# Output and up projection of a transformer layer in float32: the border between them cut at 128 tokens, the conditioning paced by progress

## The chip, the cores and the metric

The kernel runs on one core of a Trainium2 chip. The metric is device time in microseconds (us) of one execution; the profile's span is the time from the core's first instruction to its last. Five engines work side by side, each in its own program order: TensorE (PE, matrix products), VectorE (DVE), ScalarE (ACT), GpSimd (POOL) and SyncE (SP, which here issues every DMA). They wait for each other through semaphores.

## What is computed

One layer over 256 latent tokens (with 256 context tokens beside them as keys), model width 2048, everything in float32. The part around the change:

```
sh1, sc1, g1, sh2, sc2, g2 = split(silu(c) @ w_ada + b_ada, 6)    # conditioning, 2048 each
merged = g_a * (o_a @ w_br_a) + g_b * (o_b @ w_br_b)              # both attention branches
x = x + g1 * (merged @ w_out)                                     # output projection, 2048 x 2048
z = rms_norm(x, norm2_g) * (1 + sc2) + sh2                        # per token over 2048 columns
u = z @ w_up                                                      # up projection, 2048 x 11264
x = x + g2 * ((silu(conv(u)_a) * conv(u)_b) @ w_down)             # width-3 depthwise conv over tokens
out = rms_norm(x, final_norm_g)
```

The norm between the two projections needs a token's whole row of x, so no product of the up projection can start before all columns of w_out are done for its token.

## The kernel before

Every float32 operand of a large product is split into two parts of the type float32r: `hi`, a rounding cast on ACT, and `lo`, the remainder, a subtraction on DVE (`hi_lo`, `split`). A product is three matrix products, hi with hi, hi with lo and lo with hi (`mm3`). Weights come in DMAs of 1 MB into a ring of four buffers (`raw`), in one fixed order written in the generator `weights()`; `take()` hands out the next split unit and keeps two further units split ahead (`AHEAD`). There are three buffers each for `hi` and `lo`.

The order on PE is the order of the Python code. Small work (norms, softmax, evacuations, conditioning) stands in generators, the lanes of `Pace`, which adds up estimated times while the program is written: after each matmul group `tick` lets a lane take a step when the backlog that it has added up for DVE and ACT is under the lane's limit. The conditioning of sh2, sc2, g1 and g2 is such a lane (`ada_rest`): 64 loads of 1 MB of w_ada, each followed by two DVE instructions of 1024 columns (`acc<-raw,cs,acc`) that add into one row sum `acc`, and per 1024 columns a product with ones that sums over partitions. Fixed limits per stage hold it back, and `hold` stops it after 32 loads (sh2, sc2) until attention is done; g1 then runs while w_out is multiplied, g2 in the up projection.

The output projection (`w_out_group`, two column halves g) holds four PSUM banks: bank b is token tile b // 2 (128 tokens) and column piece b % 2 (512 columns). All four go through the 16 row tiles kt side by side; only the last two row tiles are done bank by bank. Behind the second half stands the border, with DVE and ACT in written order (`manual_schedule`): four times `residual` (times g1, add x, square and sum), `row_scale` (the norm's factor per token, with a power on POOL), `normed`, transposes on PE, and then per row tile `z2`: ACT writes hi, DVE writes `zf` (the same in full float32) and lo. The first 1024 columns of the up projection (`up_first`) form z2 for both token tiles as they go, in products of 256 tokens; all later parts (`up_part`, 512 columns) multiply hi and lo of z2 side by side, 512 columns at a time (`group_W`).

Earlier, at the end of the gate products, `finish(ll)` forces out what is left of the lane that prepares the latents. Its last piece, `prep_kpe`, rotates the shared key on DVE (`kr`, `kt`) and PE transposes the result before the next projection starts.

Of the kernel before, what the change touches and what calls it, by code (L numbers as in the profile page):

```python
# [32 lines left out]


# [4 lines left out]
REST_CI, REST_AFTER, REST_DMA = 1, 6.0, 6.0  # L39
GAPS = (0.0, 4.0, 10.0, 14.0, 14.0)  # L40
# [10 lines left out]
class Pace:  # L51
# [26 lines left out]
    def tick(self):  # L78
# [4 lines left out]
        while moved:  # L83
            moved = False
            for lane in list(self.lanes):
                gen, ready, limit, dma, _ = lane
                if self.pe < ready or self.left["dve"] > limit or self.left["act"] > limit or self.left["dma"] > dma:
# [63 lines left out]
def _build(tc, nc, es, a):  # L151
# [289 lines left out]
    def ada_rest():  # L441
        for vname, v, gslot in (("sh2", 3, None), ("sc2", 4, None), ("g1", 2, "K1"), ("g2", 5, "Y0")):
            for sec in range(2):
                c0 = v * D + sec * 1024
                while taken_raws[0] >= hold[0]:
                    yield 1.0
# [30 lines left out]
                else:  # L477
                    if sec == 0:
                        gb[vname] = slot(gslot, [P, D])
# [10 lines left out]
                if sec == 1:  # L490
                    ada_done.add(vname)
                yield 0.0


    hold, taken_raws = [32], [0]
    rest = ada_rest()


# [138 lines left out]

    def rows4(w, nk, c0):
# [6 lines left out]
    def weights():  # L645
# [28 lines left out]
        for g in range(2):  # L674
            yield from rows2(a["w_out"][0], KT, g * 1024, 1024)
        yield from rows2(a["w_up"][0], KT, 0, 1024)
        for c0 in up_cols[1:]:
# [8 lines left out]
    up_parts = [(0, 0, None)]  # L686
    for g in range(6):
        for half in range(2):
            for sub in range(min(8, FT - 8 * g) // 4):
                if g + half > 0:  # L690
                    up_parts.append((g, half, sub))
    up_cols = [0] + [half * FF + g * 1024 + sub * 512 for g, half, sub in up_parts[1:]]
# [29 lines left out]
    for ci in range(nch - 1):  # L722
# [4 lines left out]
        if ci == REST_CI:  # L727
            pace.add(rest, after=REST_AFTER, limit=REST_LIM, dma=REST_DMA, prio=9)
# [263 lines left out]
    pace.limit(rest, REST_LIM_B)  # L992
# [62 lines left out]
    pace.limit(rest, REST_LIM_Q)  # L1055
# [109 lines left out]
    pace.limit(rest, REST_LIM_A)  # L1165
# [3 lines left out]
    hold[0] = 48  # L1169
    pace.limit(rest, REST_LIM_W)  # L1170
# [27 lines left out]
    def w_out_group(g):  # L1198
        ps = [bank() for _ in range(4)]
        def prod(kt, b, w):  # L1200
# [5 lines left out]
        for kt in range(KT - 2):  # L1206
            w = take()
# [3 lines left out]
        w = [take(), take(1)]  # L1211
        for b in range(4):
            for k in range(2):
                prod(KT - 2 + k, b, w[k])
        yield

        def end():
            for b in range(4):
                residual(ps[b], gb["g1"], b // 2, 2 * g + b % 2, ss2)
                yield 0.0  # L1220

        if g == 0:
            pace.add(end(), limit=LIM_EVAC, prio=0)
        banks.extend(ps)

    banks = []
    run(w_out_group(0))
    run(w_out_group(1))
    while "g1" not in ada_done:
        next(rest)  # L1230
# [22 lines left out]
    def z2_parts():  # L1253
        for n in range(4):
            if n == 0:
                xh = first
            else:
                with tc.issue_after(lv_done.ins):
                    xh = [normed(t, n) for t in range(2)]
            for j in range(0, 4, 2):  # L1260
                ps = bank()
                for t in range(2):
                    for k in range(2):
                        transpose(ps[:, (2 * k + t) * P:(2 * k + t + 1) * P], xh[t][:, (j + k) * P:(j + k + 1) * P])
                for k in range(2):
                    kt = 4 * n + j + k
                    zf = tmp.tile([P, T], F32, tag="zf", bufs=1, name="zf")
                    pv = ps[:, k * T:(k + 1) * T]
                    hv, lv = z2[kt // 4][:, kt % 4, 0, :], z2[kt // 4][:, kt % 4, 1, :]
# [210 lines left out]
```

## Time and profile before

| | |
|---|---|
| three runs | 1541.64, 1546.9, 1548.05 us; median 1546.9 us |
| profiled execution | 1542.4 us, of which 1540.6 us are the span |
| mean granted clock of PE | 0.991 of full speed |
| PE busy | 1503.3 us |
| DVE, ACT, POOL busy | 1099.2, 766.5, 14.3 us |
| read from HBM | 346.84 MB, 226 GB/s over the span |

A PE that shows busy is not at its peak, since matmuls overlap and their ends are modelled; the pace of a stretch is read from the starts of its instructions. The granted clock is 1.00 at 2.4 GHz and 0.50 at 1.2 GHz.

### The profile page before, as it was taken

The page shows a single profiled execution, that of the slowest core. Times are in us where ns is not written, and L with a number is a line of the kernel's source. Part 1 is how long each engine was busy: PE and PEld are TensorE (multiplying, and loading weights), DVE is VectorE, ACT ScalarE, POOL GpSimd, SP SyncE. Part 2 cuts the span into 40 slices and gives each one's busy share as a digit, 9 for nine tenths or more (in the row PEclk, how much of TensorE's full clock was granted, in tenths as well). Part 3 has the DMA queues.
Part 4 walks back from the last instruction along what each step waited for, and adds up shares of the span by engine and source line. Part 5 has one row for each costly group of instructions (what it writes and reads, how often), then busy time and mean ns, then how long its engine had stood idle before and what let it go on. Part 6 is the DMA issues. An engine that isn't in the chain of part 4 may idle for free.

```text
span 1540.6 us, 23202 instructions
## 1 busy us (share of the span) xinstructions
PE 1503.3 (98%) x9361; PEld 1322.6 (86%) x9361; DVE 1099.2 (71%) x1553; ACT 766.5 (50%) x1145; POOL 14.3 (1%) x23
## 2 busy tenths in 40 slices
PE   6999999999999999999989999999999999999997
PEld 5788888899998988998879888888888888888885
DVE  3457686797777888698878988667666667555556
ACT  4634242355774446643446555455545545444444
POOL 0000000010000000000000000000000000000000
PEclk9999999999999999999989999999999999999999
DMA  9779888655346885478967878655555465555552
GB/s 360 244 261 337 286 309 295 247 182 194 110 142 198 276 284 187 145 285 305 343 228 269 282 257 311 209 183 182 192 192 191 165 212 181 197 197 195 193 195 79
DMA packets 123676, 350.44 MB, mean 227 GB/s; under 512 B 6718, under 2 KB 20264, under 8 KB 117040
## 3 DMA queue, kind: packets, MB, share of 16 engines
q1 hardware_dynamic: 123568, 348.96, 65.1%
q8 instruction: 73, 1.20, 0.3%
q14 instruction: 35, 0.29, 0.1%
HBM read 346.84 MB, written 2.10 MB: 226 GB/s over the span
## 4 chain that ended last, share of the span: by engine, by line
PE 94%; DVE 2%; DMA 1%; ACT 1%; issue 0%; SPq 0%; ACTq 0%; POOLq 0%; POOL 0%; DVEq 0%
PE bank L210 90%; PE bank L398 2%; PE bank L219 2%; DMA raw<-in_w_ada 1%; DVE sK L140 0%; DMA sK<-in_x 0%; DVE sX L140 0%; DVE lo L140 0%; DVE scratch L140 0%; ACT scratch L140 0%; SPq L392 0%; DVE acc L140 0%; ACT sK L140 0%; DVE sG L140 0%; ACT hi L140 0%
## 5 line engine op out<-in xcount | busy, mean ns | idle before, releaser
L140 DVE TENSOR_TENSOR lo<-raw,hi 128x1024 fp32r<-128x1024 f32 (+2 forms) x463 | 547.9, 1187 | 303.0 <-ACT hi L140 301.5
L140 ACT CAST hi<-raw 128x1024 fp32r<-128x1024 f32 (+2 forms) x463 | 471.7, 1022 | 582.9 <-PE bank L210 500.9
L210 PE MATMUL bank<-sZL,hi 128*128 128x256 f32 (+2 forms) x2528 | 540.7, 314 | 3.0 <-ACT hi L140 2.5
L210 PEld LDWEIGHTS bank<-sZL,hi 128*128 128x128 f32 (+1 forms) x2528 | 411.3, 192 | 29.4 <-issue 7.5
L210 PE MATMUL bank<-sZL,lo 128*128 128x256 f32 (+1 forms) x1648 | 389.2, 283 | 0.6 <-DVE lo L140 0.5
L210 PEld LDWEIGHTS bank<-sZL,lo 128*128 128x128 f32 (+1 forms) x1648 | 292.6, 191 | 14.7 <-DVE lo L140 1.1
L210 PE MATMUL bank<-hi,sZC 128*128 128x512 f32 (+1 forms) x816 | 261.0, 383 | 0.0
L210 PE MATMUL bank<-sX,hi 128*128 128x512 f32 (+1 forms) x896 | 235.1, 364 | 0.0
L210 PEld LDWEIGHTS bank<-hi,sZC 128*128 128x128 f32 x816 | 152.6, 188 | 29.8
L210 PEld LDWEIGHTS bank<-sX,hi 128*128 128x128 f32 x896 | 154.0, 190 | 15.7 <-issue 1.0
L140 DVE SCALAR_TENSOR_TENSOR acc<-raw,cs,acc 128x1024 f32<-128x1024 f32 x120 | 153.4, 1279 | 13.1 <-DMA raw<-in_w_ada 12.1
L210 PE MATMUL bank<-lo,sZC 128*128 128x512 f32 (+1 forms) x344 | 131.3, 382 | 0.0
L210 PEld LDWEIGHTS bank<-sX,lo 128*128 128x128 f32 x704 | 110.5, 189 | 13.6
L210 PE MATMUL bank<-sX,lo 128*128 128x256 f32 x704 | 119.9, 281 | 0.0
L210 PEld LDWEIGHTS bank<-lo,sZC 128*128 128x128 f32 x344 | 64.7, 188 | 12.5 <-DVE lo L140 0.2
L140 DVE TENSOR_TENSOR sK<-bank,sK 128x512 f32<-128x512 f32 (+1 forms) x92 | 59.6, 683 | 8.2 <-PE bank L210 6.9
L210 PE MATMUL bank<-hi,sZL 128*128 128x512 f32 x192 | 63.3, 392 | 0.0
L210 PE MATMUL bank<-sZC,hi 128*128 128x256 f32 x256 | 51.5, 288 | 1.4 <-DVE sZC L140 1.4
L210 PE MATMUL bank<-lo,sX 128*128 128x512 f32 x128 | 50.1, 391 | 0.8 <-DVE lo L140 0.8
L210 PE MATMUL bank<-hi,sX 128*128 128x512 f32 x128 | 50.2, 392 | 0.0
L140 DVE TENSOR_TENSOR sG<-bank,sG 128x512 f32<-128x512 f32 x64 | 41.8, 682 | 6.0 <-PE bank L210 6.0
L210 PEld LDWEIGHTS bank<-hi,sZL 128*128 128x128 f32 x192 | 36.1, 188 | 9.4 <-ACT hi L140 1.2
(202 smaller groups left out, 1397.4 us busy)
## 6 DMA issues: line engine op xcount, KB each, us to landing
raw<-in_w_up SPq DMA_DIRECT2D x88, 1024.0 KB, 5.0
raw<-in_w_ada SPq DMA_DIRECT2D x82, 1024.0 KB, 6.4
raw<-in_w_down SPq DMA_DIRECT2D x44, 1024.0 KB, 4.8
raw<-in_w_in SPq DMA_DIRECT2D x37, 1024.0 KB, 5.0
raw<-in_w_out SPq DMA_DIRECT2D x16, 1024.0 KB, 7.8
raw<-in_w_ada SPq DMA_DIRECT2D x16, 768.0 KB, 5.7
raw<-in_w_br_b SPq DMA_DIRECT2D x8, 1024.0 KB
raw<-in_w_br_a SPq DMA_DIRECT2D x8, 1024.0 KB, 9.3
```

Source lines behind the costliest of these rows:

```text
L140: return f(*args, **kw)
L210: PE.matmul(out, lhsT, rhs, start=start, stop=stop, skip_group_check=True)
L219: PE.transpose(out, src, ident[:n, :n])
L398: PE.matmul(ps[32 * g:32 * g + 32, :cols], cs[:, j0 + jj, :], w[:, jj, :], start=j0 + j == 0, stop=j0 + j == 14, skip_group_check=True)
```

## The change

Three things change together.

The second half of w_out runs 11 row tiles over all four banks; the weights of the last five (`KEEP`) are split into slots of their own that are free by then (G0 to G3, Y0), and the four banks are finished one after the other, 15 matmuls each. The load order of the weights follows (`rows_kept`), and `take` looks further ahead there.

Behind banks 0 and 1, which hold the first 128 tokens, their norm, their transposes and z2 of the first six row tiles are written among the matmuls of banks 2 and 3. The up projection's first part is now 512 columns wide: for the first six row tiles the two token tiles are multiplied apart (`up_joined`), the rest as in all other parts (`group_W`). `up_first` is gone.

The conditioning lane gets a limit that grows with its lag behind an even pace of 48 loads up to a point of the plan (`DUE`), g1 is summed before attention ends and only its evacuation waits for its slot, and the program asks for each half of g1 where it is needed.

```diff
+KEEP = ("G0", "G1", "G2", "G3", "Y0")
+DUE = 640.0
...
-                while taken_raws[0] >= hold[0]:
+                while vname == "g2" and vname not in slots_free:
                     yield 1.0
...
                 else:
+                    while vname not in slots_free:
+                        yield 1.0
...
+    def behind():
+        lag = 48 * (pace.pe - begin[0]) / (DUE - begin[0]) - taken_raws[0]
+        return floor[0] + max(0.0, min(1.2, 0.2 * lag))
...
+    def rows_kept(w, kt0, c0):
+        for k0, kn in halves(len(KEEP)):
+            r = load(w[(kt0 + k0) * P:(kt0 + k0 + kn) * P, c0:c0 + 1024].rearrange("(k p) c -> p k c", p=P),
+                     [P, kn, 1024])
+            for k in range(kn):
+                t = slot(KEEP[k0 + k], [P, 2, 1024], F32R)
+                hi_lo(t[:, 0, :], t[:, 1, :], r[:, k, :])
+                yield t[:, 0, :], t[:, 1, :]
...
-            pace.add(rest, after=REST_AFTER, limit=REST_LIM, dma=REST_DMA, prio=9)
+            begin[0] = pace.pe
+            pace.add(rest, after=REST_AFTER, limit=behind, dma=REST_DMA, prio=9)
...
-        for kt in range(KT - 2):
-            w = take()
+        whole = KT - (2, len(KEEP))[g]
+        for kt in range(whole):
+            w = take(AHEAD + max(0, kt - 5) if g else AHEAD)
...
+        else:
+            last_w.extend(take() for _ in KEEP)
+            last_prod.append(lambda k, b: prod(whole + k, b, last_w[k]))
...
+    def up_joined(kt, t):
+        wh = first_w[kt // 2][0]
+        mov = z2[kt // 4][:, kt % 4, :, t * P:(t + 1) * P]
+        for n, p in enumerate(up_ps):
+            mm(p.rearrange("p (h t) -> p h t", h=2)[:, :, t * P:(t + 1) * P], wh[:, kt % 2, n * P:(n + 1) * P], mov,
+               kt == 0 and t == 0, False)
...
+        last_bank(0)
+        more(1)
+        last_bank(1)
+        last_residual(0)
+        more(1)
+        last_bank(2)
+        last_residual(1)
+        more(1)
+        row_scale(0)
+        xh[0], xh[1] = [normed(0, 0)], [normed(0, 1)]
+        last_bank(3, range(3))
+        last_residual(2)
+        z2_some(xh[0], range(4), (0,))
+        last_bank(3, range(3, len(KEEP)))
+        z2_some(xh[1], (4, 5), (0,))
+        last_residual(3)
+        row_scale(1)
+        xh[0].append(normed(1, 0))
+        up_ps.extend(bank() for _ in range(4))
+        for kt in range(6):
+            up_joined(kt, 0)
+        z2_some(xh[0], range(4), (1,))
+        xh[1].append(normed(1, 1))
+        for kt in range(6):
+            up_joined(kt, 1)
+            if kt == 0:
+                z2_some(xh[1], (4, 5), (1,))
...
+            up_low(kt)
```

**PE at the border.** The names are PSUM banks on the left of the arrow, operands on the right: sX and sZC are the merged attention, sG and sY the kept weights, sZL the z2 tiles. Before, from the last product of w_out on:

```order
L210 MATMUL bank<-hi,sX_6807 128x512
L210 MATMUL bank<-lo,sX_6807 128x512
L210 MATMUL bank<-hi,sZC_6809 128x512
L210 MATMUL bank<-acc,ones 128x512 x2
L219 MATMUL bank<-ident,scratch 128x128 x8
L210 MATMUL bank<-sZL_8144,hi 128x256 x2
L210 MATMUL bank<-sZL_8144,lo 128x256
```

Now, from the third kept row tile of bank 3 on:

```order
L216 MATMUL bank<-sG_8027,sX_6860 128x512 x2
L216 MATMUL bank<-sG_8027,sZC_6862 128x512
L225 MATMUL bank<-ident,scratch 128x128 x4
L216 MATMUL bank<-sG_8042,sX_6860 128x512 x2
L216 MATMUL bank<-sG_8042,sZC_6862 128x512
L216 MATMUL bank<-sY_8047,sX_6860 128x512 x2
L216 MATMUL bank<-sY_8047,sZC_6862 128x512
L225 MATMUL bank<-ident,scratch 128x128 x2
L216 MATMUL bank<-sZL_8085,hi 128x2x128 x16
L216 MATMUL bank<-sZL_8086,hi 128x2x128 x8
L225 MATMUL bank<-ident,scratch 128x128 x4
L216 MATMUL bank<-sZL_8085,hi 128x2x128 x4
```

Transposes of the first token tile stand among the last products of w_out; 24 products follow that need this tile alone, then the transposes of the second tile.

**DVE at the border.** `sK` is x of one token tile, `st` and `r` the norm's factor, `scratch<-sK,r` is `normed`. Before, from the last residual on:

```order
L140 TENSOR_TENSOR scratch<-bank,sK_7729 128x512
L140 TENSOR_TENSOR sK_7501<-sK_7501,scratch 128x512
L140 TENSOR_SCALAR scratch<-sK_7500,r_8143 128x512
L140 TENSOR_REDUCE st<-ss_7504 128x1
L140 TENSOR_SCALAR st<-st 128x1
L140 TENSOR_SCALAR scratch<-sK_7501,r_8143 128x512
L140 TENSOR_SCALAR zf<-bank,a2col,s2col 128x256
L140 TENSOR_TENSOR sZL_8144<-zf,sZL_8144 128x256
```

Now, from behind the residual of bank 1 to the norm of the second token tile; the pair of `zf` and `sZL_8085` stands four times in a row, and the pair of `sZL_8086` twice:

```order
L146 TENSOR_TENSOR lo<-raw,hi 128x1024
L146 TENSOR_REDUCE st<-ss_7558 128x1
...
L146 TENSOR_SCALAR scratch<-sK_7554,r_8084 128x512 x2
L146 TENSOR_TENSOR scratch<-bank,sK_6954 128x512
...
L146 TENSOR_SCALAR zf<-bank,a2col,s2col 128x128
L146 TENSOR_TENSOR sZL_8085<-zf,sZL_8085 128x128
...
L146 TENSOR_TENSOR sZL_8086<-zf,sZL_8086 128x128
L146 TENSOR_TENSOR scratch<-bank,sK_6954 128x512
L146 TENSOR_TENSOR sK_7555<-sK_7555,scratch 128x512
L146 TENSOR_REDUCE st<-ss_7558 128x1
L146 TENSOR_SCALAR st<-st 128x1
L146 TENSOR_SCALAR scratch<-sK_7555,r_8084 128x512
```

The split of an up weight stands ahead of the first factor, and the residual of bank 3, the second factor and the second tile's `normed` stand behind all six pairs of z2 of the first tile.

**DVE at the end of the gate products**, ahead of the key rotation (`kr`). Before:

```order
L140 TENSOR_TENSOR lo<-raw,hi 128x1024
L140 TENSOR_TENSOR sK_5029<-scratch,sK_4953 128x512
L140 TENSOR_TENSOR lo<-raw,hi 128x768
L140 COPY kr<-bank 128x256
L140 TENSOR_TENSOR lo<-raw,hi 128x768
```

Now:

```order
L146 SCALAR_TENSOR_TENSOR acc<-raw,cs,acc 128x1024 x2
L146 TENSOR_TENSOR lo<-raw,hi 128x1024 x2
L146 TENSOR_TENSOR lo<-raw,hi 128x768
L146 SCALAR_TENSOR_TENSOR acc<-raw,cs,acc 128x1024 x2
L146 COPY kr<-bank 128x256
```

Four instructions of the conditioning now stand shortly ahead of `kr`, two of them directly.

## Rows read from the trace of the kernel before

**Rows 1.** Page, first part: busy us, share of the span, instructions, by engine.
```profile
PE 1503.3 (98%) x9361; PEld 1322.6 (86%) x9361; DVE 1099.2 (71%) x1553; ACT 766.5 (50%) x1145; POOL 14.3 (1%) x23
```

**Rows 2.** Timeline of PE at the border: start, length, instruction, count, [idle before <- releaser].
```profile
774.33 0.39 PE L210 MATMUL bank<-hi,sZC 128*128 128x512 f32 x1
...
775.01 0.39 PE L210 MATMUL bank<-hi,sZC 128*128 128x512 f32 x1
775.24 1.88 PE L210 MATMUL bank<-acc,ones 128*128 128x512 f32 x4
...
784.91 1.54 PE L219 MATMUL bank<-ident,scratch 128*128 128x128 f32 x6 [1.21 <-DVE scratch L140]
...
787.29 0.58 PE L210 MATMUL bank<-sZL,hi 128*128 128x256 f32 x1 [0.46 <-DVE sZL L140]
...
792.37 0.47 PE L210 MATMUL bank<-sZL,hi 128*128 128x256 f32 x2
```

**Rows 3.** Timeline of DVE at the border and shortly behind it.
```profile
776.91 0.69 DVE L140 TENSOR_TENSOR scratch<-bank,sK 128x512 f32<-128x512 f32 x1 [1.44 <-ACT sK L140]
...
778.25 0.68 DVE L140 TENSOR_TENSOR scratch<-bank,sK 128x512 f32<-128x512 f32 x1
...
784.37 0.49 DVE L140 TENSOR_SCALAR scratch<-sK,r 128x512 f32<-128x512 f32 x1 [0.68 <-POOL r L239]
...
786.24 0.54 DVE L140 TENSOR_SCALAR zf<-bank,a2col,s2col 128x256 f32<-128x256 f32 x1 [1.38 <-ACT sZL L140]
...
798.18 0.55 DVE L140 TENSOR_SCALAR zf<-bank,a2col,s2col 128x256 f32<-128x256 f32 x1
...
799.36 0.54 DVE L140 TENSOR_SCALAR zf<-bank,a2col,s2col 128x256 f32<-128x256 f32 x1 [0.18 <-ACT sZL L140]
```

**Rows 4.** Timeline of ACT in the same stretch.
```profile
782.60 0.63 ACT L140 ACTIVATE scratch<-sK 128x512 f32<-128x512 f32 x1 [0.86 <-DVE sK L140]
...
785.64 0.56 ACT L140 ACTIVATE sZL<-bank,s2col,a2col 128x256 fp32r<-128x256 f32 x1 [2.32 <-PE bank L219]
...
792.45 1.05 ACT L140 CAST hi<-raw 128x1024 fp32r<-128x1024 f32 x1 [3.05 <-PE bank L210]
...
798.76 0.57 ACT L140 ACTIVATE sZL<-bank,s2col,a2col 128x256 fp32r<-128x256 f32 x1 [1.36 <-DVE zf L140]
```

**Rows 5.** The chain that ended last: start, length, what; behind the border.
```profile
795.91 5.76 PE bank L210 x48
```

**Rows 6.** Windows of 1 us: busy us of five engines, PE clock granted, DMA share, GB/s.
```profile
475.00:476.00 1.00, 1.00 (x8) 1.00 (x7) 1.00 (x2) 1.00 (x4) 0.00 (x0) 0.54 0.00 0
...
782.00:783.00 1.00, 0.00 (x0) 0.00 (x0) 0.96 (x2) 0.40 (x1) 0.00 (x0) 0.64 0.20 74
```

**Rows 7.** Groups by shape, whole run: count | busy us, mean ns | idle before.
```profile
L140 DVE TENSOR_TENSOR scratch<-sK,sY 128x128 f32<-128x128 f32 x4 | 1.0, 281 | 0.0
```

**Rows 8.** Timeline of PE in the up projection, two row tiles of group_W.
```profile
898.37 0.64 PE L210 MATMUL bank<-sX,lo 128*128 128x256 f32 x4
...
899.78 0.63 PE L210 MATMUL bank<-sX,lo 128*128 128x256 f32 x4
```

**Rows 9.** Timeline of DVE at the end of the gate products.
```profile
466.63 0.96 DVE L140 TENSOR_TENSOR lo<-raw,hi 128x768 fp32r<-128x768 f32 x1 [0.83 <-ACT hi L140]
469.10 0.43 DVE L140 COPY kr<-bank 128x256 f32<-128x256 f32 x1 [1.52 <-PE bank L219]
```

**Rows 10.** Waits, 460 to 476: who <- for whom: us in total, times, longest.
```profile
PE bank L219 <- DVE scratch L140: 2.5, 1, 2.5
```

**Rows 11.** Groups of DVE, 385 to 465 us, by shape.
```profile
L140 DVE TENSOR_TENSOR lo<-raw,hi 128x1024 fp32r<-128x1024 f32 x18 | 22.0, 1222 | 13.2 <-ACT hi L140 13.2
...
L140 DVE SCALAR_TENSOR_TENSOR acc<-raw,cs,acc 128x1024 f32<-128x1024 f32 x2 | 2.6, 1282 | 0.0
```

**Rows 12.** One window, 385 to 465 us; columns as in rows 6.
```profile
385.00:465.00 80.00, 79.90 (x640) 78.02 (x639) 58.35 (x99) 60.38 (x103) 2.02 (x3) 1.00 0.38 122
```

**Rows 13.** Waits, 640 to 776 us, the w_out stage in it.
```profile
PE bank L210 <- DVE lo L140: 0.8, 1, 0.8
```

More of the change, by code (lines that the diff above doesn't have):

```diff
@@ L1251, in _build @@
     z2 = [slot(x, [P, 4, 2, T], F32R) for x in ("ZL0", "ZL1", "X2", "X3")]
[L1253 to L1256, printed above, removed]
-            else:
[L1258 to L1269, printed above, removed]
-                    ACT.activation(hv, pv, AF.Identity, bias=s2col[:, kt:kt + 1], scale=a2col[:, kt:kt + 1])
-                    if kt % 4 == 3:
-                        ACT.activation(zf, pv, AF.Identity, bias=s2col[:, kt:kt + 1], scale=a2col[:, kt:kt + 1])
-                    else:
-                        DVE.tensor_scalar(out=zf, in0=pv, scalar1=a2col[:, kt:kt + 1], scalar2=s2col[:, kt:kt + 1],
-                                          op0=ALU.mult, op1=ALU.add)
-                    op = DVE.tensor_sub(lv, zf, hv.bitcast(F32))
-                    if kt == 0:
-                        lv_done = op
-                yield
@@ new lines, in z2_some @@
+    def z2_some(xh, kts, ts):
+        c0, cn = ts[0] * P, len(ts) * P
+        ps = bank()
+        for i, kt in enumerate(kts):
+            for t in ts:
+                transpose(ps[:, i * cn + t * P - c0:i * cn + (t + 1) * P - c0], xh[t][:, (kt % 4) * P:(kt % 4 + 1) * P])
+        for i, kt in enumerate(kts):
+            zf = tmp.tile([P, T], F32, tag="zf", bufs=1, name="zf")[:, 0:cn]
+            pv = ps[:, i * cn:(i + 1) * cn]
+            hv, lv = (z2[kt // 4][:, kt % 4, h, c0:c0 + cn] for h in range(2))
+            ACT.activation(hv, pv, AF.Identity, bias=s2col[:, kt:kt + 1], scale=a2col[:, kt:kt + 1])
+            if kt % 2 and cn == T:
+                ACT.activation(zf, pv, AF.Identity, bias=s2col[:, kt:kt + 1], scale=a2col[:, kt:kt + 1])
+            else:
+                DVE.tensor_scalar(out=zf, in0=pv, scalar1=a2col[:, kt:kt + 1], scalar2=s2col[:, kt:kt + 1],
+                                  op0=ALU.mult, op1=ALU.add)
+            DVE.tensor_sub(lv, zf, hv.bitcast(F32))
@@ L1325, in up_part @@
         c0 = (half * FF + g * 1024 + sub * 512) // P
-        ps = [bank() for _ in range(4)]
-        for k2 in range(0, KT, 2):
+        if c0 == 0:
+            ps = up_ps
+        else:
+            ps = [bank() for _ in range(4)]
+        for k2 in range(6 if c0 == 0 else 0, KT, 2):
             wh, wl = take()
@@ L1330, in up_part @@
                 kt = k2 + k
+                if c0 == 0 and kt == 6:
+                    xh[3] = [normed(t, 3) for t in range(2)]
+                if c0 == 0 and kt < KT - 4:
+                    z2_next(kt + 4)
                 group_W(ps, wh[:, k, :], wl[:, k, :], flat(z2[kt // 4][:, kt % 4]), kt == 0, kt == KT - 1)
@@ L1352, in up_part, with more @@
         evacs["up"] = pace.add(end(), limit=LIM_EVAC, prio=0)
-    zgen = z2_parts()
-    with tc.manual_schedule(engines={ENG.DVE, ENG.Activation}):
-        for b in range(4):
-            residual(banks[4 + b], gb["g1"], b // 2, 2 + b % 2, ss2)
-            if b == 2:
-                row_scale(0)
-        first.append(normed(0, 0))
-        row_scale(1)
-        first.append(normed(1, 0))
-        next(zgen)
-        prepare(3)
-    hold[0] = 64
+    xh = {}
+    first_w, up_ps = [], []
+    def more(n):
+        for _ in range(n):
+            prepare(1)
+            first_w.append(ready.pop(0))
```

101 lines of the change are left out of this document (52 added, 49 removed).

## The prediction

> **What bounds the kernel now.** I read the page first: PE is busy 1503.3 of 1540.6 us [rows 1], so only about 37 us are idle, and a change that leaves PE's work alone can win only there, in half-clock time, or in the fixed cost of a matmul. Then I read PE's timeline at the border. The last product of w_out starts at 775.01; the two products for g1 end at 775.24 + 1.88 = 777.12; matmuls run at full pace again from 792.37 [rows 2]. In these 15.25 us PE does eight transposes and 24 matmuls of 256 columns. Full pace is (775.01 - 774.33) / 3 = 0.227 us for a matmul of 512 columns [rows 2], 5.76 / 48 = 0.12 us for one of 256 [rows 5], and I take 0.11 us for a transpose, an estimate from its half width against the 0.12. That work is worth 0.88 + 2.88 = 3.76 us, so the border **loses 15.25 - 3.76 = 11.5 us**: PE waits for a chain of residuals, norm and z2 on DVE and ACT, and then works at half clock. The granted clock fell inside the window of 782 to 783, after some 5 us without a matmul [rows 6].
>
> Two smaller places matter. At the end of the gate products PE waited 2.5 us for DVE [rows 10], and the clock fell right behind it, at 475 [rows 6]. In the w_out stage it waited 0.8 us for a `lo` [rows 13].
>
> **The border, step by step.** Times below count from the first kept matmul. PE needs 15 x 0.227 = 3.4 us per bank, so the banks end at 3.4, 6.8, 10.2 and 13.6 if nothing interferes.
>
> The prices: a residual on DVE 778.25 - 776.91 = 1.34 [rows 3]; from the start of its square on ACT to the start of `normed`, 784.37 - 782.60 = 1.77, of which 0.75 are ACT's part and 1.02 the row factor through POOL (the cut is an estimate) [rows 3, 4]; `normed` 0.49 [rows 3]; the cast of an up weight 1.05 [rows 4] and its `lo` 1.2 [rows 11].
>
> z2 with 128 columns is in no row. ACT took 0.56 for 256 columns [rows 4], DVE's `zf` 0.54 [rows 3]. I take 0.45 and 0.41; the bounds are half and all of these, 0.28 to 0.56 and 0.27 to 0.54. `lo` of 128 columns is 0.28, from a tensor_tensor of that size [rows 7]. The rows also show how row tiles follow each other: `zf` ends at 798.73, ACT's next read of that bank starts at 798.76 and ends at 799.33, the next `zf` starts at 799.36 [rows 3, 4]. The two engines alternate, so I take 0.45 + 0.41 + 2 x 0.03 = 0.92 us per row tile. The Trainium skill ("PSUM — Partial Sum Buffer", section "PSUM bank collisions raise a hardware error") says that no two engines may touch one bank at once, two readers included. It speaks against four row tiles in one bank, as the change packs them; the rows agree. Without the alternation only DVE's 0.41 + 0.28 + 0.04 = 0.73 would count per row tile, 8 x 0.19 = 1.5 us less over the eight that follow in a row, and the sum below would be 1543.5.
>
> - **First tile's norm.** Bank 1's residual runs 6.95 to 8.4, its square to 9.15. Then stand the third up weight's cast on ACT (to 10.2) and its `lo` on DVE (to 11.4), and only behind them the row factor: `normed` is ready at 12.95. PE wants it at 12.25, behind nine matmuls of bank 3: **0.75 us wait**. The other weight splits are hidden beside banks.
> - **First tile's z2.** Bank 2's residual follows on DVE (to 14.75), its square on ACT (to 15.5), then ACT's first z2. The first row tile is whole at 16.7; PE, through with the last transposes at 15.0, **waits 1.7**. Six row tiles at 0.92, the fifth partly overlapped because it has another bank, end at 21.15. PE's 24 matmuls (2.9 us) stretch to 21.65: **2.05 of waits**.
> - **Second tile's norm.** Bank 3 was done long before, but on DVE its residual stands behind all six z2: 21.15 to 22.5, square and factor, `normed` ready at 24.85. **PE waits 3.25.**
> - **Second tile's z2.** Four transposes, ACT, DVE: first row tile at 27.3, **1.2 of waits**. One group of four matmuls, then PE's next instruction is a transpose that needs the second tile's second `normed`, which DVE does behind three more row tiles: 30.55. **PE waits 2.45.** From then on it has work.
>
> The waits sum to 11.4 us. Every stretch like it in rows fell to half clock, and between 15 and 30.6 PE is mostly idle, so I add half-clock time: about 0.65 us for the four transposes and four matmuls on the way, and 2.55 behind: the clock came back 792.37 - 787.29 = 5.1 us after steady work began [rows 2], and half of such a stretch is lost. The new border loses 11.4 + 0.65 + 2.55 = 14.6 against 11.5: **+3.1 us**.
>
> **What else changes.** The first up part: 384 matmuls of 256 columns (46.1 us) become 32 groups of 899.78 - 898.37 = 1.41 us [rows 8], 45.0, plus 24 matmuls from the cut, 24 x (0.24 - 0.227) = 0.3: **-0.8**. The g1 products on PE stay, elsewhere.
>
> The conditioning: no load and no DVE instruction is added, 32 `acc` instructions move. About 12 of them, 12 x 1.28 = 15.4 us, go to where 2 of them stood between 385 and 465 us [rows 11] (14 now stand between the 100th and the 120th `lo` in DVE's order, 2 before). DVE has 80 - 58.35 = 21.65 us free there [rows 12], so most is covered. Without that cover each would be worth up to its 1.28. At the end of that stretch it is not: two `acc`, 2.56 us, stand between the `lo` that ended at 467.6 and `kr` at 469.10 [rows 9]. `kr` starts at 470.15, and all that PE waits for behind it is DVE work: **+1.1** (0 if DVE runs that much ahead, +2.6 if nothing is covered or the load is late). Behind `kr` stand the gates' evacuations and the next `lo`, which PE needs only after that same wait. In return the 0.8 us wait in the w_out stage, where `acc` was dense, should go: **-0.85** (0 if not). The loads go ahead of attention weights in SP's queue; ring and order stay, and the stretch has a DMA share of 0.38 [rows 12], so I take 0 there. The kept weights are split beside 30 us of matmuls.
>
> **The sum.** 1542.4 + 3.1 - 0.8 + 1.1 - 0.85 = **1545 us**, against the profiled execution (span 1540.6 and 1.8 around it), which lies 4.5 under the median of the three runs shown, so a difference is better judged beside runs of the same chip. The three runs lie 6.4 us apart: 0.5% (7.7 us) is about what a measurement of this kernel can tell from no change.
>
> **Rivals.**
> - *The clock holds.* The matmuls and transposes between the waits keep it at 1.00; then only the waits count, 11.9 with quicker transposes, +0.4 instead of +3.1: **1542.3**. For it: no wait alone is longer than 3.25 us. Against it: 2.5 us were enough at 475 [rows 6, 10]. The Trainium skill ("TensorE: Matmul & The Clock Gate", Part 1) describes the gate as set by how busy PE has recently been, not by one gap; by that rule this is open, and no row shows such a mix.
> - *The chain hides.* If the second tile's norm is ready when PE gets there (17.9 on my scale instead of 24.85), nearly all waits but the first go, and the border loses some 3.7: 1542.4 - 7.8 - 0.8 - 0.85 = **1533**. For it: the first tile's chain does run beside banks 2 and 3. Against it: seven us of DVE and ACT work stand between, in written order, at prices from rows.
> - *The paced conditioning makes attention late* (slower). Weights are split two units ahead, 2 x 2.88 us; where softmax steps, evacuations and `acc` put DVE more than 5.8 us behind, every further `acc` reaches PE. For it: 13.2 of DVE's free time in the stretch are waits for a cast [rows 11] and may not be usable, which leaves 8.5 of 15.4. Then 7 us on top, and the wait at `kr` another 2.6: **1555**. Against it: the lane steps only at a small backlog.
>
> **Chances.** Forecast 0.47, the clock holds 0.20, the chain hides 0.18, attention late 0.15. The first two are within 0.5%: same 0.67, faster 0.18, slower 0.15. The unknown sizes (z2 -2.5 to +1.9 over eight row tiles, clock -2.7, `kr` -1.1 to +1.5, w_out +0.85) put the forecast alone between 1539 and 1550; with most of the other two cases, and up to 4.5 for the profiled execution against the median, the range is 1535 to 1553.
>
> **What would show it.** Right: PE idle in five pieces behind bank 3, the longest ahead of the second tile's transposes, for `scratch`; granted clock 0.50 for about 10 us there; up parts all at 1.41 us per row tile; `kr` about 1 us later and PE's wait there over 3; no wait on `lo` in the w_out stage. Wrong: one short wait at the border, or a clock of 1.00 throughout it (first two rivals); waits of PE for `hi` or `lo` between 385 and 465 (third).

## The result and the profile after

The changed kernel takes **1565.7 us** (median of four runs, 1563.8 to 1567.9) against 1547.2 for the kernel before on the same chip: a ratio of 1.0133, 95% interval 1.0113 to 1.0153. It is **slower by 1.3%** (18.5 us between the two medians), where I had forecast no change that can be told. The profiled execution after has a span of 1564.5 us, 23.9 more than the one before.

The first view to read is the page's busy times. Before, PE worked 1503.3 us [rows 1]:

```profile
span 1564.5 us, 23036 instructions
PE 1512.1 (97%) x9257; PEld 1321.6 (84%) x9257; DVE 1103.9 (71%) x1572; ACT 770.5 (49%) x1160; POOL 14.2 (1%) x23
```

PE has fewer instructions than before and is busy 8.8 us longer: matmuls at half clock. The rest is waits. To see where, I cut the span in two. The *head* ends with the last matmul of w_out (before: with g1's products behind it, 775.24 + 1.88 = 777.1 [rows 2]; after: the first kept matmul plus 60 x 0.227 = 13.6). The *tail* is the rest of the span. This row of PE's timeline after is the first kept matmul:

```profile
783.15 0.62 PE L216 MATMUL bank<-sG,sX 128*128 128x512 f32 x2
```

So the head ends at 783.15 + 13.6 = 796.75, which is **19.6 us later** than before, and the tail is 1564.5 - 796.75 = 767.75 against 1540.6 - 777.12 = 763.5, **4.3 us longer**. The border, on which most of my prediction went, is the small part.

Where in the head? I paired matmuls of the same operands in the two traces: the later one is 5.8 us late from 256 to 361 us (before's time), 20.0 late at 463. So 14.2 us are lost in the gate stage, where I had looked for 1.1. With the 4.3 of the tail that makes 18.5, the difference of the medians; the 5.8 us before 256 us are near the 4.8 by which before's profiled execution beats its median, and no run here shows them to be the change's. PE's waits there, from 385 to 470, where before shows not one:

```profile
PE bank L216 <- DVE scratch L146: 5.5, 1, 5.5
PE bank L216 <- DVE sK L146: 1.7, 1, 1.7
PE bank L216 <- DVE rr L146: 1.1, 2, 0.9
```

PE's timeline shows the long one: the products of ones with the squares of cq (the sums for cq's norm).

```profile
409.33 1.04 PE L225 MATMUL bank<-ident,scratch 128*128 128x128 f32 x8
415.87 1.44 PE L216 MATMUL bank<-ones,scratch 128*128 128x1 f32 x6 [5.50 <-DVE scratch L146]
```

DVE's and ACT's timelines in these 5.5 us:

```profile
409.40 1.28 DVE L146 SCALAR_TENSOR_TENSOR acc<-raw,cs,acc 128x1024 f32<-128x1024 f32 x1
...
410.72 1.21 DVE L146 TENSOR_TENSOR lo<-raw,hi 128x1024 fp32r<-128x1024 f32 x1
...
411.96 0.67 DVE L146 TENSOR_TENSOR sK<-bank,sK 128x512 fp32r<-128x512 f32 x1
412.55 1.27 DVE L146 SCALAR_TENSOR_TENSOR acc<-raw,cs,acc 128x1024 f32<-128x1024 f32 x1
413.74 0.68 DVE L146 TENSOR_TENSOR scratch<-scratch 128x512 f32<-128x512 f32 x1
414.34 0.68 DVE L146 TENSOR_TENSOR sK<-bank,sK 128x512 fp32r<-128x512 f32 x1
415.12 0.69 DVE L146 TENSOR_TENSOR scratch<-scratch 128x512 f32<-128x512 f32 x1
```

```profile
411.75 0.62 ACT L146 ACTIVATE scratch<-sK 128x512 f32<-128x512 f32 x1
...
414.46 0.63 ACT L146 ACTIVATE scratch<-sK 128x512 f32<-128x512 f32 x1 [0.49 <-DVE scratch L146]
```

The squares (ACT, `scratch<-sK`) and their sums (DVE, `scratch<-scratch`) stand in order behind heads' work, a weight's `lo` and two `acc`; the product is reached before they are. Before, the same sum on DVE and the same product on PE stood 28 us apart, and PE did not wait:

```profile
404.18 0.68 DVE L140 TENSOR_TENSOR scratch<-scratch 128x512 f32<-128x512 f32 x1
432.95 0.95 PE L210 MATMUL bank<-ones,scratch 128*128 128x1 f32 x8
```

So more than DVE's queue has changed. Counted in the two traces, 120 of the matmuls with a weight's `hi` or `lo` ran on PE between that last sum and the product before, and none after; the product stands 144 such matmuls (17 us at 0.12) earlier in PE's order. Its lane may take the step 2 us of planned matmul time behind the sums, and the limits on the backlog decide when it does: before, they let it come much later. The new pace has moved that step too. Behind the wait the clock is down: these windows show PE's busy time and granted clock (columns: window, length, PE, PEld, DVE, ACT, POOL, clock, DMA share, GB/s).

```profile
411.00:416.00 5.00, 0.13 (x1) 0.13 (x1) 4.72 (x7) 3.60 (x8) 0.00 (x0) 0.69 0.59 189
416.00:424.00 8.00, 8.00 (x36) 7.60 (x37) 3.44 (x7) 1.45 (x3) 0.70 (x1) 0.55 0.40 145
385.00:465.00 80.00, 72.71 (x543) 68.89 (x542) 58.55 (x102) 56.14 (x101) 1.71 (x2) 0.94 0.46 159
```

The third window answers to [rows 12]: DVE is busy 58.55 us of 80, as before (58.35). It isn't full. It does ten more `acc` (12 against 2), and other work comes later.

The border after, on PE's timeline:

```profile
795.99 0.66 PE L225 MATMUL bank<-ident,scratch 128*128 128x128 f32 x4 [0.44 <-DVE scratch L146]
...
799.74 0.71 PE L216 MATMUL bank<-sZL,hi 128*128 128x256 f32 x4 [1.49 <-DVE sZL L146]
800.67 0.71 PE L216 MATMUL bank<-sZL,hi 128*128 128x256 f32 x4 [0.23 <-DVE sZL L146]
...
807.92 0.66 PE L225 MATMUL bank<-ident,scratch 128*128 128x128 f32 x4 [2.40 <-DVE scratch L146]
809.99 1.19 PE L216 MATMUL bank<-sZL,hi 128*128 128x256 f32 x4 [1.41 <-DVE sZL L146]
813.11 0.69 PE L225 MATMUL bank<-ident,scratch 128*128 128x128 f32 x2 [1.93 <-DVE scratch L146]
...
831.37 1.19 PE L216 MATMUL bank<-sX,hi 128*128 128x512 f32 x4 [0.41 <-DVE sX L146]
...
838.10 1.19 PE L216 MATMUL bank<-sX,hi 128*128 128x512 f32 x4 [0.78 <-DVE sX L146]
```

The pieces stand where I forecast them, the longest ahead of the second tile's transposes. They are shorter: down to 813.11 the waits come to 8.1 us (one more of 0.23 at 801.61), where I had 11.4. What is missing of them went into matmuls at half clock, which set in earlier than I had it, among the first tile's 24 matmuls (columns as above):

```profile
802.00:805.00 3.00, 2.92 (x14) 2.65 (x13) 2.55 (x8) 0.46 (x1) 0.00 (x0) 0.50 0.03 8
808.00:818.00 10.00, 6.66 (x31) 6.16 (x32) 6.53 (x16) 3.79 (x7) 0.00 (x0) 0.54 0.07 28
```

Two more waits, 0.41 and 0.78, come later, for z2 blocks that I had not priced.

### The profile page after: what moved, and what is told of

Read it like the earlier page. It is cut to its first block, busy times and chain, and to the rows that moved or that the text cites. A ratio compares the mean times of both kernels' runs of the same rounds, so it can differ in the third digit from the quotient of the medians.

```text
span 1564.5 us, 23036 instructions
## 1 busy us (share of the span) xinstructions
PE 1512.1 (97%) x9257; PEld 1321.6 (84%) x9257; DVE 1103.9 (71%) x1572; ACT 770.5 (49%) x1160; POOL 14.2 (1%) x23
## 5 line engine op out<-in xcount | busy, mean ns | idle before, releaser
L146 DVE TENSOR_TENSOR lo<-raw,hi 128x1024 fp32r<-128x1024 f32 (+2 forms) x458 | 542.1, 1187 | 306.7 <-ACT hi L146 303.4
L216 PE MATMUL bank<-sZL,hi 128*128 128x256 f32 (+1 forms) x2488 | 536.4, 317 | 5.9 <-DVE sZL L146 3.4
L216 PEld LDWEIGHTS bank<-sZL,hi 128*128 128x128 f32 x2488 | 405.6, 193 | 34.7 <-issue 8.7
L216 PE MATMUL bank<-sZL,lo 128*128 128x256 f32 (+1 forms) x1648 | 381.8, 284 | 0.6 <-DVE lo L146 0.6
L216 PE MATMUL bank<-hi,sZC 128*128 128x512 f32 (+1 forms) x796 | 253.4, 383 | 0.0
L216 PE MATMUL bank<-sX,hi 128*128 128x512 f32 (+1 forms) x832 | 229.6, 379 | 1.2 <-DVE sX L146 1.2
L216 PEld LDWEIGHTS bank<-sX,hi 128*128 128x128 f32 x832 | 145.0, 189 | 18.7 <-DVE sX L146 1.6
L216 PE MATMUL bank<-sX,lo 128*128 128x256 f32 x704 | 112.0, 281 | 0.0
L146 DVE TENSOR_TENSOR sK<-bank,sK 128x512 f32<-128x512 f32 (+1 forms) x92 | 59.5, 683 | 11.4 <-PE bank L216 7.7
L146 ACT COPY scratch<-bank 128x256 f32<-128x256 f32 (+2 forms) x100 | 32.5, 397 | 26.5 <-PE bank L404 17.2
L216 PE MATMUL bank<-hi,sX 128*128 128x512 f32 x108 | 42.4, 393 | 0.0
```

The source lines that it names most:

```text
L146: return f(*args, **kw)
L216: PE.matmul(out, lhsT, rhs, start=start, stop=stop, skip_group_check=True)
```

## The experiments

My theory was that the pace of the conditioning loses the time and the border is nearly even; the rival, that the border loses it. Each ratio is against runs of the kernel before on the same chip (medians 1544.3 to 1547.2); it comes from all the runs, and the quotient of the medians differs a little (1.0120 for the changed kernel). Head and tail are worked out from each profile as above (us). In single executions heads of one order of work differ by several us, and tails of one border by up to 2.5.

| Run | Median us | Ratio to before (95%) | Head | Tail |
|---|---|---|---|---|
| before | 1547.2 | 1 | 777.1 | 763.5 |
| after | 1565.7 | 1.0133 (1.0113-1.0153) | 796.8 | 767.8 |
| e1_border_only | 1570.6 | 1.0166 (1.0148-1.0183) | 801.4 | 768.5 |
| e2_pace_only | 1562.7 | 1.0104 (1.0080-1.0129) | 801.4 | 760.7 |
| e3_no_lag_in_gates | 1550.3 | 1.0043 (1.0028-1.0059) | 784.0 | 768.1 |
| e4_cq_later | 1556.8 | 1.0076 (1.0061-1.0092) | 787.8 | 767.0 |
| e5_lag_after_gates | 1553.3 | 1.0059 (1.0040-1.0077) | 784.7 | 766.4 |
| e6_border_reordered | 1553.6 | 1.0041 (1.0025-1.0057) | 789.9 | 762.2 |
| e7_one_bank | 1554.1 | 1.0057 (1.0040-1.0074) | 788.2 | 765.0 |
| e8_old_border_lag_late | 1549.0 | 1.0029 (1.0014-1.0043) | 789.8 | 760.9 |
| e9_no_lag | 1573.7 | 1.0173 (1.0155-1.0191) | 805.6 | 767.8 |
| e10_best_border | 1565.5 | 1.0121 (1.0105-1.0137) | 802.6 | 762.2 |
| e11_old_border_no_lag | 1545.4 | 0.9993 (0.9981-1.0004) | 778.9 | 763.5 |
| e12_lag_first_part_only | 1573.5 | 1.0165 (1.0143-1.0186) | 797.4 | 768.7 |
| e13_lag_q_and_attention | 1555.7 | 1.0072 (1.0058-1.0087) | 786.2 | 767.6 |
| e14_best_border_lag_qa | 1548.3 | 1.0015 (1.0001-1.0028) | 784.8 | 761.3 |
| e15_old_border_lag_qa | 1546.8 | 1.0010 (0.9996-1.0024) | 782.8 | 759.8 |
| e16_best_border_lag_ea | 1552.5 | 1.0051 (1.0037-1.0066) | 788.4 | 761.2 |
| e17_best_border_late_products | 1553.1 | 1.0050 (1.0036-1.0063) | 787.5 | 763.7 |
| e18_old_border_late_products | 1538.5 | 0.9956 (0.9944-0.9968) | 772.8 | 759.6 |

**The two parts alone.** The first keeps the new border and puts the conditioning back:

```diff
-        return floor[0] + max(0.0, min(1.2, 0.2 * lag))
+        return floor[0]
-                while vname == "g2" and vname not in slots_free:
+                while vname in ("g1", "g2") and vname not in slots_free:
```

> The new border with the conditioning as it was before (fixed limits, g1's loads only after attention). Theory (the loss lies in the pace of the conditioning, the border's net is the +1.5 us of the prediction): before plus 0 to 4 us, a ratio of 1.000 to 1.003, and all PE work up to 640 us at the same times as before. Rival (the border loses the time): before plus 15 to 24 us, 1.010 to 1.015.

The second puts `behind`, `floor` and `slots_free` into the kernel before and leaves its border as it was.

> The old border and the old first up part, with the conditioning on the new pace and g1 summed early. Theory: before plus 20 to 24 us, 1.013 to 1.016, with PE waiting some 5 us for the product of cq's squares near 410 us. Rival (the border loses the time): before plus 0 to 4 us.

Both are slower: 1.0166 and 1.0104. The second bears the theory out, though under its size (1.013 to 1.016): its own border got 2.8 us shorter (the tail in the table), since g1 is early. The first refutes it as I put it, and its trace says why:

```profile
784.97 3.78 PE L216 MATMUL bank<-acc,ones 128*128 128x512 f32 x4 [19.32 <-DVE acc L146]
```

The new border, as written, asks for the whole of g1 ahead of the kept matmuls, since every kept bank's residual takes it; before, the same product stood behind all of w_out, and the sums were ready just then. So **the border and the pace are one change**: the border makes g1 due earlier, and the pace is what it costs to have it there.

**Where the pace costs.** Two edits of the changed kernel: no lag in the gates' stage, and a later place for the product that waited.

```diff
-        return floor[0] + max(0.0, min(1.2, 0.2 * lag))
+        return floor[0] + max(0.0, min(1.2, 0.2 * lag)) * (floor[0] != REST_LIM_B)
```

> The changed kernel, but between the end of the last chunk and the end of the gates the limit is the fixed 0.6 again, with nothing added for the lag. Theory (the 14 us between 385 and 463 us come from the acc that the lag lets in there): 12 to 16 us less than the changed kernel, before plus 6 to 11 us, 1.004 to 1.007; what is not taken there is taken later at no more than 3 us. Rival (they come from elsewhere, as from the transfers): within 3 us of the changed kernel, 1.011 to 1.015.

```diff
         yield from squares([flat(cq[:, 2 * i:2 * i + 2, :]) for i in range(3)], sq)
-        yield 2.0
+        yield 10.0
```

> The changed kernel, with the product of cq's squares held back by 10 us of matmul time behind its squares in place of 2. The number of acc in the stretch stays. Theory (the loss there is one place, PE reaching that product before DVE and ACT have the squares): the 5.5 us wait and the half clock behind it go, 8 to 11 us less than the changed kernel, before plus 9 to 16 us, 1.006 to 1.010. Rival (DVE's load as such, which would only make PE wait elsewhere): within 3 us of the changed kernel, 1.011 to 1.015.

Both came out as the theory has them: 1.0043 and 1.0076 against 1.0133, about 14 and 9 us less. In the second the `acc` are still there, and PE is idle for 2 us of 80, where the changed kernel is idle for 7 and then works near half clock for 8 and more (window 385 to 465 of the run with cq's product later; the same window of the changed kernel stands above):

```profile
385.00:465.00 80.00, 77.95 (x616) 74.57 (x615) 66.23 (x106) 61.33 (x107) 0.70 (x1) 1.00 0.55 184
```

So DVE did have room for the `acc`. They cost what they did because, under the new pace, one product came right behind its sums, whose queue they lengthened. The two runs part these causes: without the lag in the gates the product is back in its old place, 120 matmuls behind the last sum; with the later place it is 44 behind, with 14 `acc` still in the stretch, and that wait is gone. By which step of the plan the pace moved the product, I did not follow up. The next product of this kind then waited in its place: 5.0 us at 480.8 for kpp's `scratch`, where the changed kernel waits 3.3.

**The lag elsewhere, and the border without it.** The lag only behind the gates, with three borders: as changed, reordered, and reordered with one bank; and the old border with the same lag.

```diff
-        return floor[0] + max(0.0, min(1.2, 0.2 * lag))
+        return floor[0] + max(0.0, min(1.2, 0.2 * lag)) * (floor[0] not in (REST_LIM, REST_LIM_B))
```

> The changed kernel with the fixed limits 0.65 and 0.6 until the gates end, and the lag added only from the q_up stage on; g1 may still be summed before attention ends. Theory (the border's net is +1 to +2 us if g1's sum is there when the kept matmuls begin, and the early lag and the lag in the gates were the rest of the loss): before plus 0 to 4 us, 1.000 to 1.003, with no wait of PE for the g1 products. Rival (the border itself costs more than it gives, as the run with the old conditioning would have it if its 19 us wait were only a part): before plus 8 us or more, over 1.005.

```diff
         last_residual(1)
-        more(1)
         row_scale(0)
         xh[0], xh[1] = [normed(0, 0)], [normed(0, 1)]
-        last_bank(3, range(3))
+        last_bank(3, range(2))
         last_residual(2)
-        z2_some(xh[0], range(4), (0,))
-        last_bank(3, range(3, len(KEEP)))
-        z2_some(xh[1], (4, 5), (0,))
+        z2_tile(range(4), 0)
+        last_bank(3, range(2, len(KEEP)))
         last_residual(3)
+        z2_tile((4, 5), 0)
         row_scale(1)
+        more(1)
         xh[0].append(normed(1, 0))
+        xh[1].append(normed(1, 1))
```

(`z2_tile` is `z2_some` with 128 columns, its row tiles dealt out to two banks in turn; the second tile's calls follow the first tile's matmuls.)

> As the run with the lag after the gates, and the border's order changed: the third up weight's split stands behind the first tile's row factor and last, bank 3's residual ahead of the fifth and sixth row tile, both of the second tile's first two normed blocks ahead of its z2, and four row tiles of z2 share two banks in turn. Theory (waits at the border come from DVE's written order and from ACT and DVE taking turns at one bank): PE is at full work some 22 to 24 us after the first kept matmul in place of 30, 5 to 8 us less than the run with the lag after the gates, before minus 3 to 6 us, 0.996 to 0.998. Rival (the chain is bound by latencies that stay, or the clock takes it back): within 2 us of the run with the lag after the gates.

> As the run with the border reordered, but the four row tiles of z2 in one bank again. Theory (ACT and DVE take turns at one bank, 0.94 us per row tile against about 0.73 with two): 1 to 2 us more than with two banks, and ACT's reads start only where zf ends. Rival (the turns have another cause): the same time, and the same spacing of row tiles with two banks.

> The old border and the old first up part, with the conditioning of the run with the lag after the gates. With that run it prices the new border alone. Theory: the new border costs 0.5 to 3 us net against this one, and this one is within 3 us of before, 0.998 to 1.002. Rival (the new border gains once its conditioning is in time): this one slower than the run with the lag after the gates by 2 us or more.

Here the whole times blur, since heads of the same order of work came out at 784.7 to 789.9; the tails tell more, within the 2.5 us above. Reordered with two banks the tail is 762.2, with one 765.0, as changed 766.4: the order can give back 4. But the old border's tail is 760.9: with g1 summed early, its product and a part of its wait leave the border too. The rival for the first of the four holds in part (1.0059, over the 1.000 to 1.003 of the theory). The reordered border missed its forecast as well (1.0041, not 0.996 to 0.998), and so did the old border with the same lag (1.0029, over 0.998 to 1.002); its 0.3% under the changed border is more than the 0.5 to 3 us that I had given the new border. One bank against two, 1.0057 and 1.0041, is in the direction of the theory, but the intervals overlap.

The banks: DVE's `zf` of successive row tiles, with one bank and then with two:

```profile
789.13 0.41 DVE L146 TENSOR_SCALAR zf<-bank,a2col,s2col 128x128 f32<-128x128 f32 x1 [0.20 <-ACT sZL L146]
790.07 0.41 DVE L146 TENSOR_SCALAR zf<-bank,a2col,s2col 128x128 f32<-128x128 f32 x1 [0.20 <-ACT sZL L146]
```

```profile
790.81 0.41 DVE L146 TENSOR_SCALAR zf<-bank,a2col,s2col 128x128 f32<-128x128 f32 x1
791.65 0.41 DVE L146 TENSOR_SCALAR zf<-bank,a2col,s2col 128x128 f32<-128x128 f32 x1
```

0.94 us per row tile in turns at one bank, 0.84 with two, where the waits for ACT are gone. The Trainium skill ("PSUM — Partial Sum Buffer", section "PSUM bank collisions raise a hardware error") would have it so that two banks free the two engines of each other; the rows agree, but the gain is 0.10, not the 0.19 that I had worked out from DVE's own durations.

**Is it the lag, or the earlier sums?** The fixed limits throughout, with three borders, and the lag in the first part alone:

```diff
-        return floor[0] + max(0.0, min(1.2, 0.2 * lag))
+        return floor[0]
```

> The changed kernel with the fixed limits throughout and nothing added for the lag; g1 may be summed before attention ends, as in the change. Theory (all of the loss behind the border's +1.5 is the lag): before plus 0 to 4 us, 1.000 to 1.003, no wait of PE at the product of cq's squares and none for a weight's lo over 1.5 us in the last third before the border. Rival (summing g1 before attention ends costs by itself): over 1.005.

(For the last of the four the factor is `* (floor[0] == REST_LIM)`. The improved border moves `more(1)` right behind the first tile's `normed`, and the squares of banks 2 and 3 behind the z2 reads.)

> The fixed limits throughout, g1 summed before attention ends, and the reordered border improved: the third up weight is split right behind the first tile's normed blocks, and the squares of banks 2 and 3 stand on ACT behind the z2 reads that PE waits for first. Theory: the 3.6 us wait for the third weight's cast falls under 1.5, PE is at full work some 2 us earlier than in the run with the border reordered, and with no loss from the lag the kernel is faster than before by 2 to 6 us, 0.996 to 0.999. Rival (reordering only moves the waits): before plus 0 to 4 us, as the run without lag.

> The old border and the old first up part; the only difference to before is that g1's loads and sums go on during attention, under the fixed limits. Theory (the product for g1, 1.9 us on PE, and a part of the wait for the residuals leave the border): before minus 2 to 5 us, 0.997 to 0.999. Rival (what the border gains is lost in attention): within 1.5 us of before.

> The changed kernel with the lag counted only until the gates begin, the fixed limits behind. Theory (the early lag delays a pair of w_ada loads behind which PE waits at about 111 and 198 us, then half clock): 2 to 6 us more than the run without lag. Rival (the 5.8 us before 250 us were a difference between two single executions): within 1.5 us of the run without lag.

All four theories missed; the rivals of the first, third and fourth hold. That g1 may be summed during attention does nothing by itself: under the fixed limits the old border stays at 0.9993, its `acc` where they were, and the new borders stop for g1 again, 19.7 to 20.4 us each. Only the lag brings the sums forward, and not in the first part alone (20.4 there). And the 5.8 us that the changed kernel was late by 250 us are not shown to be the lag's: the medians with the early lag and without are 1573.5 and 1573.7, while over the profiled executions the lateness at 286 us lies between -1.4 and 9.7.

**Which later stage.** The lag only in q_up and attention (`floor[0] in (REST_LIM_Q, REST_LIM_A)`) with three borders, and one run with it in the first part and attention:

> The changed kernel with the lag counted in the q_up and attention stages alone. Theory (behind attention DVE is filled to over 80% and the lag's extra acc there stand ahead of a lo that PE needs): g1's product is in time, the 2.7 us wait at about 697 us and the half clock behind it go, 3 to 5 us less than the run with the lag after the gates, before plus 3 to 6 us. Rival (the loss lies in q_up and attention): within 1.5 us of the run with the lag after the gates, before plus 7 to 9 us.

> The improved border with the lag in the q_up and attention stages alone. Theory (the border's order costs 5 us that can be had back): 4 to 6 us less than the same lag with the changed border, before minus 2 to plus 2 us. Rival (the clock takes back what the shorter waits give): within 2 us of it.

> The old border and the old first up part with the lag in the q_up and attention stages alone. Theory: g1's product leaves the border, which then takes 4.5 us less than before, as in the run with the old border and the lag after the gates; the lag costs 4 to 6 us; so within 2 us of before, and 5 us less than the changed border with the same lag. Rival: slower than before by 4 us, as with the lag after the gates.

> The improved border with the lag counted until the gates begin and in the attention stage, not in the q_up stage. Theory (the sums cost least where DVE is least busy, which is 605 to 645 us and the time before the gates): 0 to 3 us less than the improved border with the lag in q_up and attention. Rival (attention is where they cost, by its chain of exponentials): 2 us or more above it.

The first: the 2.7 us wait at 697 did go, but not the time (1.0072 against 1.0059, intervals that overlap): the theory falls, and where the later lag costs is not shown; no wait that is left from 470 to 770 is over 2.6 us. The second bears the theory out and goes beyond its 4 to 6 us: 1.0015 against 1.0072 with the same lag, so the border's order was worth some 8 us, 6.3 of them in the tail. The third: 1.0010, so with equal lag **the changed border costs 0.6%, 9 us, against the old one** (tails 767.6 and 759.8), and the improved one nothing that can be told. The two other pairs with equal lag give 0.3% each: the changed kernel against the pace alone (tails 767.8 and 760.7), and the lag after the gates with both borders (766.4 and 760.9). So the price is 0.3 to 0.6%, 5.5 to 7.8 us in the tails, and more than the 4.3 against before, whose border still had g1's product and its wait in it. The fourth: 1.0051, against the theory; PE waits 3.9 us for a `lo` at 696.

**Products with more room.** The lag as in the last two, and two more products further behind their work:

```diff
                     ACT.copy(sb[0:64, :], ps[0:64, :])
-                    yield 1.5
+                    yield 8.0
         yield from prep_cq()
-        yield from prep_ckv()
         yield from prep_kpe()
+        yield from prep_ckv()
-        yield 2.5
+        yield 6.0
         for i, s in enumerate((ph, pl)):
```

> The improved border with the lag in q_up and attention, and two products moved to a later place among the matmuls: the transposes for kpp are prepared between cq's and ckv's part and stand 6 us of matmul time behind their last step in place of 2.5, and the conditioning's own transposes 8 us in place of 1.5. Theory (a fixed distance that is too short is what makes these waits): the waits of 3.0 us at 474 and of 0.6 and 1.7 us at 583 to 589, and a half clock of 3.4 us, go; 4 to 7 us less than the improved border with that lag, before minus 2 to 6 us, 0.996 to 0.999. Rival (DVE's backlog, which would stop PE at the next place): within 2 us of it.

> The same two moves with the old border and the old first up part, under the same lag. Theory: 4 to 7 us less than the old border with that lag, before minus 3 to 6 us, 0.996 to 0.998, and within 2 us of the run with the improved border and the same moves. Rival (DVE's backlog): within 2 us of the old border with that lag.

With the old border: 0.9956 (0.9944 to 0.9968), 1538.5 us, **faster than both kernels**, and some 8 us under the same lag without the moves (the theory had 4 to 7). PE's waits from 385 to 830 are down to these (7.3, 2.2, 1.9, 0.5 and 0.3 us in all without the moves):

```profile
PE bank L221 <- DVE scratch L142: 3.6, 2, 2.2
PE bank L212 <- DVE lo L142: 1.4, 1, 1.4
PE bank L212 <- DVE sZL L142: 0.5, 1, 0.5
PE bank L221 <- ACT scratch L142: 0.2, 1, 0.2
```

With the improved border the same moves made it slower, 1.0050. The waits aimed at are gone there too, but g1 is late again, most likely since holding the conditioning's own product back delays its lane (with the old border the same moves put g1's last product at 765.4 in place of 759.1, where nothing needs it yet). PE's waits from 385 to 830 are led by

```profile
PE bank L216 <- DVE acc L146: 9.5, 1, 9.5
```

How much of the gain of the run with the old border would come without any lag, from the moves alone, was not tried.

## Why the prediction was wrong

- **The border's steps were right.** From the first kept matmul: first transposes 12.84 (I said 13.0), first z2 matmul 16.6 (16.7), 0.94 per row tile (0.92), the second tile's transposes 24.8 (24.85), its first matmul 26.8 (27.3), its second block 30.0 (30.55). The granted clock was 0.54 from 808 to 818, and low for 10 us there, as said; the 0.50 from 802 to 805 I did not have. The rivals that the clock holds and that the chain hides fell; the Trainium skill ("TensorE: Matmul & The Clock Gate", Part 1) ties the gate to how busy PE has recently been, and this stretch, where no wait is over 2.4 us, agrees.
- **The border's sum was low**: +3.1 - 0.8 = +2.3 against a tail longer by 4.3. Counted at the prices of the rows, PE lost 14.1 us from the end of w_out to full pace at 819.1, where I had 14.6, so the shortfall lies behind that: 2.5 us up to 866, from where the two traces keep step. The two later waits are 1.2 of it; the rest is open. Two sums in the prediction are off by less: on its own times (16.95 us from 13.6 to 30.55, with 4.46 us of work) the loss is 12.5, not 11.4 + 0.65, and 32 x 1.41 is 45.1, which makes the first up part -0.65. The size is also not fixed: eight executions with this border have tails of 766.4 to 768.7 and 6.8 to 13.6 us of half clock at it.
- **The step that failed is the conditioning.** "DVE has 21.65 us free there, so most is covered", and of the loads "I take 0 there": the terms were +1.1 at `kr` and -0.85 in w_out, where the head shows 19.6. The -0.85 came true (0.2 us of waits for `lo` from 700 to 783), and PE's wait behind `kr` was 3.3 instead of 2.5. But I counted DVE's free time as a sum over 80 us, and asked of only one product, at the end, what stands ahead of it. The product of cq's squares, the conditioning's own product (1.7 us for `sK`) and the `rr` products stand in the same stretch, and of none of them did I ask how far behind its work it stands. In place of cover the runs showed 14 us that go when the lag is taken out there, 9 of them at one product, which the pace had moved from 28 us behind its sums to right behind them.
- **What I counted at nothing in the change: that the border makes g1 due some 14 us earlier.** I wrote of "32 `acc` that move" without asking what forces them to. Without the lag the price is a stop of 19 to 20 us.
- The slower rival, "The paced conditioning makes attention late", had the stretch right and DVE's order as the cause. It looked for waits on a weight's `lo` and priced them at 7 + 2.6 us; the waits were on a norm's sums, and dearer by the half clock behind them. I gave it 0.15.
- The sum was made on the profiled execution, 1542.4, which was 4.8 under the median of before's runs. Its early part is among the quickest seen: most of the other executions are later by 286 us, by up to 9.7, in an order of work that hardly differs.

## What to carry to other kernels

Free time of an engine, summed over a stretch, covers nothing by itself: what counts is the queue ahead of each instruction that PE will wait for, so walk every product in the stretch, in the new order, and ask how far behind its inputs' work it stands; a pace for one lane can move the steps of the others. When a step is moved earlier, list what it reads and when that is ready; whatever must hurry for it is a cost of the move. And cut the trace in a head and a tail at the moved place before explaining a total.

## What was not expected of the hardware

In two executions, several short waits cost more time at half clock than one longer one. In the run with the improved border and no lag the waits at the border are 1.26, 0.23, 0.42 and 0.77 us, and the clock in four windows of 3, 4, 4 and 4 us is

```profile
806.00:809.00 3.00, 1.60 (x12) 1.25 (x10) 2.69 (x7) 0.91 (x3) 0.00 (x0) 1.00 0.16 66
809.00:813.00 4.00, 2.68 (x13) 1.81 (x11) 2.09 (x7) 1.30 (x5) 0.56 (x1) 0.60 0.52 219
813.00:817.00 4.00, 3.90 (x19) 3.93 (x20) 2.52 (x7) 1.89 (x5) 0.00 (x0) 0.54 0.00 0
817.00:821.00 4.00, 3.17 (x28) 3.00 (x26) 3.48 (x6) 1.96 (x4) 0.00 (x0) 1.00 0.31 76
```

With the border reordered but one wait of 3.56 us, PE was slow for half as long:

```profile
797.00:801.00 4.00, 3.35 (x14) 2.92 (x14) 2.64 (x7) 1.01 (x3) 0.56 (x1) 0.58 0.20 82
801.00:805.00 4.00, 3.23 (x26) 3.07 (x26) 3.36 (x10) 2.80 (x7) 0.00 (x0) 0.99 0.00 0
```

So 1.5 us less of waiting (3.5 against 5.1 in all at the border) brought no shorter tail, 762.2 in both. It does not come out the same each time: another execution of the improved border (e16, waits of 1.26, 0.49, 0.61 and 1.09 us) was slow for a shorter time, with a clock of 0.50 from 798 to 801 and 0.96 from 801 to 803, and a tail of 761.2. What sets the length of the slow stretch is not shown here.
